# Experts with few rows: float32 weights used as loaded, two 64-column products side by side

## The chip, the cores and the metric

The kernel runs on one core of a Trainium2 chip. The metric is the device time of one execution in microseconds: the median of three runs is 1269.22 us (1267.71 to 1270.82).

## What is computed

One decoder layer on 1024 tokens of width 1024. The part that matters here is the last one, a mixture of 32 experts. Each token is sent to two experts; the kernel computes only those rows. All arithmetic is to float32 accuracy.

```python
def hier_moe(h, rg_w, rg_b, re_w, re_b, w_gate, w_up, w_down):
    ...                                   # group top-1, then expert top-2 inside it
    y = jnp.zeros_like(h)
    for e in range(N_EXPERTS):            # 32 experts
        he = jax.nn.silu(h @ w_gate[e]) * (h @ w_up[e])   # (1024 x 256) each
        y = y + comb[:, e:e + 1] * (he @ w_down[e])       # (256 x 1024)
    return y
```

One expert's weights are 1024x256 (gate), 1024x256 (up) and 256x1024 (down), 3 MB in float32.

## The kernel before

Attention, gating and the output product come first (lines 155 to 1090). The expert part, `moe` (line 1574), works through 35 units: the 32 experts, those after the sixth sorted by how many tokens they have, and a second half unit for the three experts in `PAIRS`. A unit has 128 slots for tokens, or 64 if it is a second half or its expert is one of the 13 in `SMALLS` (9, 11, 13, ... 29, 30, 31). Units 0 to 8 all have 128 slots; from expert 9 on, large and small ones alternate.

A unit goes like this. GpSimd gathers the token rows by an indirect DMA (`gather`). TensorE transposes them and `tokens` splits them into a high and a low part: ScalarE writes `xh` as float32r (a shortened float32), VectorE the rest `xl`. `gate_up` multiplies by gate and up weights, `down` by the down weights, ScalarE scales the result into `y`, and GpSimd adds it to the rows of `acc` in memory by an accumulating indirect DMA (`scatter`).

Weights come in pieces of 128x1024 values, 0.5 MB: four for gate and up together, two for down, so 192 for the experts. `plan` (line 155) lists them with the engines of their split, `fetch` loads a piece on the SP queue into a page `wr`, `presplit` splits it into two pages, `wh` and `wl` (`split`, line 138: line 132 or 136 writes the high part on ScalarE or GpSimd, line 140 the low part on VectorE or GpSimd). With a piece given as "a", ScalarE writes `wh` and VectorE `wl`. Down pieces of experts 0 to 27 go by `DOWN = "gp"`: for the first GpSimd writes `wh` and VectorE `wl`, for the second ScalarE writes `wh` and GpSimd `wl`. The pages come from one pool of 41; a load waits on the SP queue until a page is free.

A product of two split numbers takes three float32r matmuls (`mm3`, line 143). In a unit of 64 slots `xh` and `xl` stand beside each other as 128 columns, so two matmuls do for `gate_up`: all 128 columns by `wh` (line 1495) and the 64 of `xh` by `wl` (line 1494), 16 for the eight blocks of 128; the two halves are added while they are turned (line 1506). `down` takes 12 in either kind of unit.

The last two experts (30, 31) don't scatter: their results stay in SBUF and are added by matmuls in `finish` (line 1699). The order on each engine is set by the framework's scheduler, from the order of the code and its own costs; pools and semaphores decide the rest.

Of the kernel before, what the change touches and what calls it, by code (L numbers as in the profile page):

```python
# [10 lines left out]
F32 = mybir.dt.float32  # L11
F32R = mybir.dt.float32r
BF16 = mybir.dt.bfloat16
I32 = mybir.dt.int32
U32 = mybir.dt.uint32
AF = mybir.ActivationFunctionType
ALU = mybir.AluOpType
# [72 lines left out]
class Kern:  # L90
# [25 lines left out]

    def era(self):

        return self.const.tile([P, 448], F32, name=self.name("era"), tag="era")

    def temp(self, shape, dt):

# [32 lines left out]
    def plan(self):  # L155
        I = self.I
        win = I["w_in"][0]
        W = []

        def cols(src, kt, c0, w, eng="a", k0=0):  # L160
            ap = src[k0 * P : (k0 + kt) * P, c0 : c0 + w].rearrange("(k p) c -> p k c", p=P)
            W.append(([P, kt, w], lambda t: [self.nc.sync.dma_start(t, ap)], eng))

        cols(win, KT, C_KI, 72, "q")
        for j in range(4):
            cols(win, KT, C_QI + j * P, P, self.QI[j])
# [12 lines left out]
        for j in range(4):
            cols(win, KT, C_Q + j * P, P)  # L180
        for d in range(4):
            cols(I["w_proj_a"][0], 4, d * 256, 256)
        kw = D // self.OW
        for c in range(D // self.OW):
            for j in range(KT // kw):
                cols(I["w_out"][0], kw, c * self.OW, self.OW, "a", j * kw)

        def gu(get):
            for j in range(4):

                def ld(t, j=j):
                    wg, wu, _ = get()
                    for z, w in enumerate((wg, wu)):
                        self.nc.sync.dma_start(t[:, :, z * 256 : (z + 1) * 256], w[j * 256 : (j + 1) * 256, :].rearrange("(k p) f -> p k f", p=P))

                W.append(([P, 2, 512], ld, "a"))

        def dn(get, eng):
            for f in range(2):
                W.append(([P, D], lambda t, f=f: self.nc.sync.dma_start(t, get()[2][f * P : (f + 1) * P, :]), eng[f]))  # L200

        gets = [self.expert(e) if e < FIXED else self.ordered(e) for e in range(NE)]
        self.units = [(e, z) for e in range(NE) for z in range(1 + (e in PAIRS))]
        for what, u in self.sequence():
            e, z = self.units[u]
            if z == 0 and what == "gu":
                gu(gets[e])
            elif z == 0:
                dn(gets[e], self.DOWN if e < NE - self.LAST else "aa")
        self.W = W  # L210
        self.raws, self.hls = [], []
        self.pos = 0
        self.urgent = {}
        self.LD, self.LS = self.EARLY_LD, 1
# [43 lines left out]
    def presplit(self, n):  # L258
        n = min(n, len(self.W))
        self.fetch(n)  # L260
        while len(self.hls) < n:
            i = len(self.hls)
            shape, _, eng = self.W[i]
            h = self.page(shape, F32R, "wh")
            l = self.page(shape, F32R, "wl")
            with ExitStack() as es:
                for ins in self.urgent.values():
                    es.enter_context(self.tc.issue_after(ins))
                self.split(eng, h, l, self.raws[i])
            self.raws[i] = None  # L270
            self.hls.append((h, l))
# [658 lines left out]
    def merge(self):  # L930
# [38 lines left out]
        self.acc = self.dram.tile([T, D], F32, name="acc")  # L969
        late = self.era()  # L970
        self.lg = late[:, : 8 * 40].rearrange("p (t c) -> p t c", t=8)
        self.olists = late[:, 8 * 40 :].rearrange("p (z e) -> p z e", z=4)
        self.r2 = self.cst([P, 8], F32, "r2")
        ss = self.small([P, 8, NC], F32, "ss2", bufs=1)
        xs = []
# [112 lines left out]
    ROUTE_PAGES = (1, 0)  # L1088
    RINGS = (3, 1, 2)
    WRITES = ["scalar"] * 13 + ["sync"] * 3  # L1090
    DOWN, LAST = "gp", 4
    XAHEAD = 4
    EARLYFETCH = {(1, 0): 12, (1, 2): 16, (1, 4): 22, (1, 6): 28}
    EARLYSPLIT = {(1, 2): 4}
# [4 lines left out]
    def router_consts(self):  # L1099
# [26 lines left out]
        self.islot, _ = iota("islot", [P, P], [[1, P]])  # L1126
        self.itile, _ = iota("itile", [P, 8], [[128, 8]])
        self.icol, _ = iota("icol", [P, 1], [[0, 1]], cm=1)

        self.places = self.cst([NE, 2, NE], F32, "places")  # L1130
        for z in range(2):
# [183 lines left out]
    def order(self):  # L1315

        nc, bc = self.nc, self.bc
        V = nc.vector
        t = self.arena()
        nt = self.ps1([P, NE + 1], "nt", tag="a")  # L1320
        nc.tensor.matmul(nt[:, :NE], lhsT=self.oneb, rhs=self.Mc[:, 8, :], start=True, stop=True)
        nc.tensor.matmul(nt[:NE, NE:], lhsT=self.Mc[:, 8, :], rhs=self.oneb[:, 0:1], start=True, stop=True)
        key, more, PO = t([P, NE]), t([P, NE]), t([P, NE])
        own, rank, rows = t([P, 1]), t([P, 1]), t([P, 1])
        e = slice(0, NE)
        dyn, tie, fixed = (self.cols[:, z : z + 1] for z in range(3))

        V.scalar_tensor_tensor(key, nt[:, :NE], float(NE), self.ties, op0=ALU.mult, op1=ALU.add)
        V.tensor_tensor(key, key, self.dyn, ALU.mult)
        V.scalar_tensor_tensor(own[e], nt[e, NE:], float(NE), tie, op0=ALU.mult, op1=ALU.add)  # L1330
        V.tensor_scalar(more[e], key[e], own[e], None, op0=ALU.is_gt, op1=ALU.add, accum_out=rank[e])
        V.tensor_scalar(rank[e], rank[e], dyn, fixed, op0=ALU.mult, op1=ALU.add)
        V.tensor_scalar(PO[e], self.places[:, 0, :], rank[e], None, op0=ALU.is_equal)

        ep = self.ps1([1, NE], "eid", tag="a")
        nc.tensor.matmul(ep, lhsT=self.icol[e], rhs=PO[e], start=True, stop=True)
        self.eid = self.cst([1, NE], I32, "eid")
        V.tensor_copy(self.eid, ep)
        V.tensor_copy(rows[e], nt[e, NE:])
        self.ordered_state = rows[e], rank[e], PO[e]  # L1340
        yield

        tp = self.ps1([NE, 3, P], "lt", tag="a")
        for z in range(3):
            nc.tensor.transpose(tp[:, z, :], self.lists[:, z, :], self.ident)
        lt = self.page([NE, 5, P], F32, "lt")
        nc.scalar.activation(lt[:, :3], tp, AF.Copy)

        for z in range(2):
            nc.scalar.activation(lt[:, 3 + z].rearrange("e (r s) -> e r s", r=2), tp[:, 1 - z, :HALF].unsqueeze(1).to_broadcast([NE, 2, HALF]), AF.Copy)  # L1350
        op = self.ps1([P, 5, NE], "ol", tag="a")
        for z in range(5):
            nc.tensor.matmul(op[:, z, :], lhsT=lt[:, z, :], rhs=PO[:NE], start=True, stop=True)
        o = self.olists
        self.tokp = self.cst([P, NE], I32, "tokp")
        V.tensor_copy(self.tokp, op[:, 0, :])
        V.tensor_copy(o, op[:, 1:5])
        self.rsp, self.wsp, self.rsd, self.tokd = (o[:, z, :] for z in range(4))
        yield

    def route_overflow(self):
# [103 lines left out]
    def tokens(self, xg):  # L1465
# [14 lines left out]
        self.hurry("x", *self.lastsplit)  # L1480
        return (x2.rearrange("p k r s -> p k (r s)"),) if m == HALF else (xh, xl)

    def gate_up(self, x, r, piece):

        nc = self.nc
        pp = self.ps1([P, 512], "gu", tag="b")
        half = len(x) == 1
        for j in range(4):
            h, l = piece()
            for k in (2 * j, 2 * j + 1):  # L1490
                if half:
# [66 lines left out]

    def scatter(self, tok, y):

        self.nc.gpsimd.indirect_dma_start(out=self.acc, out_offset=bass.IndirectOffsetOnAxis(ap=tok, axis=0), in_=y[: tok.shape[0]], in_offset=None, bounds_check=T - 1, oob_is_err=False, compute_op=ALU.add)  # L1561

    def spread(self, places):

# [9 lines left out]
    def moe(self):  # L1574
# [5 lines left out]
        def lists(u):  # L1580
            e, z = units[u]
            if z:
                c = slice(PAIRS.index(e), PAIRS.index(e) + 1)
                return self.tok2[:HALF, c], self.rs2d[:, c], self.ws2[:HALF, c]
            if e in SMALLS:
                return self.tokp[: LIMITS[e], e : e + 1], self.rsd[:, e : e + 1], self.wsp[:HALF, e : e + 1]
            if e < FIXED:
                return tuple(v[:, e : e + 1] for v in (self.tok, self.rs, self.ws))
# [19 lines left out]

        self.xring = [[self.page([P, KT, P], F32R, n) for n in ("xh", "xl")] for _ in range(2)]
        self.yring = []  # L1610
        X, G = {}, {}
        seq = self.sequence()
        rows, ys = [], []
        ovf = self.route_overflow()
        for step in range(n + 2):
# [9 lines left out]
                u = len(rows)  # L1625
                rows.append(self.gather(self.tok[:, u : u + 1] if u < FIXED else lists(u)[0], self.xg[u % self.NXG][: halves(u) * HALF]))
            if step < n:
                X[step] = self.tokens(rows[step])
            if step == 0:
                self.route_factors()  # L1630
                order = self.order()
# [3 lines left out]
            while seq and seq[0][1] < step - (seq[0][0] == "dn") and seq[0][1] in (X if seq[0][0] == "gu" else G):  # L1635
                what, u = seq.pop(0)
                tok, r, ws = lists(u)
                if what == "gu":
                    G[u] = self.gate_up(X.pop(u), r, pieces(u, what))
                    continue  # L1640
                if u == n - self.SPREAD:
                    self.kept = self.spread((NE - 2, NE - 1))
# [134 lines left out]
```

## Time and profile before

| what | value |
|---|---|
| median of 3 runs | 1269.22 us |
| profiled execution | 1266.41 us, its span 1264.6 us |
| TensorE busy in the span | 1141.6 us (90%) |
| VectorE busy | 985.7 us (78%) |
| ScalarE busy | 608.9 us (48%) |
| GpSimd busy | 443.2 us (35%) |
| memory traffic | 190.69 MB in packets, 151 GB/s on average |
| mean granted TensorE clock | 0.962 of full speed |

Busy times count compute instructions only. Matmul ends are modelled and overlap the next start, so what one matmul costs is read from the distance of two starts. In the names, the tile before the arrow is written by those behind it; `wr`, `wh`, `wl` are pages of weights, `xt`, `xh`, `xl` the tokens of a unit, `gu` and `y` its two products in PSUM, `kb` small tiles between the two, `gut` and `ht` the turned gate and up values. A waiting engine is shown with what released it last.

### The profile page before, as it was taken

The page shows a single profiled execution, that of the slowest core. Times are in us where ns is not written, and L with a number is a line of the kernel's source. Part 1 is how long each engine was busy: PE and PEld are TensorE (multiplying, and loading weights), DVE is VectorE, ACT ScalarE, POOL GpSimd, SP SyncE. Part 2 cuts the span into 40 slices and gives each one's busy share as a digit, 9 for nine tenths or more (in the row PEclk, how much of TensorE's full clock was granted, in tenths as well). Part 3 has the DMA queues.
Part 4 walks back from the last instruction along what each step waited for, and adds up shares of the span by engine and source line. Part 5 has one row for each costly group of instructions (what it writes and reads, how often), then busy time and mean ns, then how long its engine had stood idle before and what let it go on. Part 6 is the DMA issues. An engine that isn't in the chain of part 4 may idle for free.

```text
span 1264.6 us, 17817 instructions
## 1 busy us (share of the span) xinstructions
PE 1141.6 (90%) x5892; PEld 922.0 (73%) x5892; DVE 985.7 (78%) x1724; ACT 608.9 (48%) x1048; POOL 443.2 (35%) x406
## 2 busy tenths in 40 slices
PE   4999999989999989899999899877988788999993
PEld 3789888878888867799888788755765555666662
DVE  7444988999999994798888713768999879777875
ACT  6324642222222214687773413236657465666773
POOL 5100141510111110344425412235675784675511
PEclk7999999999999999999999999979899899999997
DMA  7301031312322220000047647868799788998936
GB/s 216 84 17 51 1 84 34 100 51 86 107 74 84 80 70 18 1 2 1 1 143 232 237 139 282 270 222 258 242 282 268 242 254 264 290 326 250 313 113 241
DMA packets 148144, 190.69 MB, mean 151 GB/s; under 512 B 16514, under 2 KB 119466, under 8 KB 148051
## 3 DMA queue, kind: packets, MB, share of 16 engines
q1 hardware_dynamic: 134226, 156.85, 38.5%
q0 software_dynamic: 8784, 21.16, 7.0%
q10 hardware_dynamic: 5040, 11.54, 2.4%
q8 instruction: 47, 0.77, 0.3%
q14 instruction: 47, 0.38, 0.1%
HBM read 164.61 MB, written 33.07 MB: 156 GB/s over the span
## 4 chain that ended last, share of the span: by engine, by line
PE 53%; DVE 24%; issue 7%; DMA 6%; ACT 5%; POOL 3%; SPq 1%; DVEq 0%; POOLq 0%; ACTq 0%
DVE wl L140 6%; PE pj L145 6%; PE pj L147 6%; PE pj L146 6%; DVE junk L546 5%; DMA wr<-w_up 4%; PE xo L146 2%; PE xo L147 2%; PE xo L145 2%; DVE S L878 2%; PE y L147 2%; PE y L145 2%; PE gu L146 2%; PE y L146 2%; PE gu L1495 1%
## 5 line engine op out<-in xcount | busy, mean ns | idle before, releaser
L140 DVE TENSOR_TENSOR wl<-wr,wh 128x1024 fp32r<-128x1024 f32 x212 | 327.2, 1561 | 46.3 <-ACT wh L132 25.8
L132 ACT ACTIVATE wh<-wr 128x1024 fp32r<-128x1024 f32 x206 | 212.1, 1054 | 60.4 <-PE pj L146 28.5
L546 DVE TENSOR_SCALAR_CACHE_REDUCE junk<-idx,cand 128x384 bf16<-128x384 f32 (+2 forms) x198 | 187.0, 944 | 6.8 <-POOL idx L509 1.0
L145 PE MATMUL pj<-hT,wh 128*128 128x512 f32 (+1 forms) x464 | 179.8, 387 | 2.5 <-ACT wh L132 2.5
L147 PE MATMUL pj<-hT,wl 128*128 128x512 f32 (+1 forms) x464 | 178.6, 385 | 0.0
L146 PE MATMUL pj<-hT,wh 128*128 128x512 f32 (+1 forms) x464 | 178.3, 384 | 0.0
L145 PEld LDWEIGHTS pj<-hT,wh 128*128 128x128 f32 x464 | 88.0, 190 | 20.1 <-ACT wh L132 2.7
L147 PEld LDWEIGHTS pj<-hT,wl 128*128 128x128 f32 x464 | 87.9, 190 | 16.8
L146 PEld LDWEIGHTS pj<-hT,wh 128*128 128x128 f32 x464 | 87.8, 189 | 16.7
L140 POOL TENSOR_TENSOR wl<-wr,wh 128x1024 fp32r<-128x1024 f32 (+1 forms) x30 | 85.7, 2856 | 13.8 <-ACT wh L132 12.8
L146 PE MATMUL gu<-wl,xh 128*128 128x512 f32 x152 | 65.5, 431 | 21.4 <-DVE wl L140 21.3
L711 POOL TENSOR_TENSOR yt<-yt,sb 128x1024 f32<-128x1024 f32 x8 | 20.1, 2512 | 169.7 <-ACT sb L719 169.7
L886 POOL TENSOR_SCALAR P<-P,pair 128x128 f32<-128x128 f32 (+3 forms) x64 | 48.1, 752 | 88.1 <-DVE pair L885 77.9
L136 POOL TENSOR_SCALAR wh<-wr 128x1024 fp32r<-128x1024 f32 (+1 forms) x36 | 48.4, 1346 | 54.8 <-ACT kih L457 17.4
L719 ACT ACTIVATE sb<-pj 128x512 f32<-128x512 f32 x32 | 19.0, 594 | 100.5 <-PE pj L147 100.5
L1561 POOL DMA_INDIRECT acc<-y,tokp x24 | 47.2, 1966 | 52.3 <-ACT y L1551 23.5
L145 PE MATMUL gu<-wh,xh 128*128 128x512 f32 x152 | 63.6, 418 | 1.0 <-ACT wh L132 0.7
L147 PE MATMUL y<-wh,kb 128*128 128x512 f32 (+1 forms) x140 | 58.7, 420 | 4.1 <-DVE kb L140 4.1
L147 PE MATMUL gu<-wh,xl 128*128 128x512 f32 x152 | 62.2, 409 | 0.0
L145 PE MATMUL y<-wh,kb 128*128 128x512 f32 (+1 forms) x140 | 59.1, 422 | 3.4 <-ACT kb L132 2.1
L146 PE MATMUL y<-wl,kb 128*128 128x512 f32 (+1 forms) x140 | 58.2, 416 | 0.0
L506 DVE SCALAR_TENSOR_TENSOR idx<-rl,era,idx 128x384 f32<-128x384 f32 (+5 forms) x42 | 39.8, 947 | 20.1 <-ACT rl L502 18.9
(434 smaller groups left out, 2904.2 us busy)
## 6 DMA issues: line engine op xcount, KB each, us to landing
wr<-w_gate SPq DMA_DIRECT2D x128, 256.0 KB, 5.3
wr<-w_up SPq DMA_DIRECT2D x128, 256.0 KB, 5.7
wr<-w_down SPq DMA_DIRECT2D x64, 512.0 KB, 5.7
wr<-w_in SPq DMA_DIRECT2D x33, 512.0 KB, 4.3
x<-x SPq DMA_DIRECT2D x8, 512.0 KB, 7.2
sga<-sb ACTq DMA_DIRECT2D x8, 512.0 KB, 4.5
ybg<-yt POOLq DMA_DIRECT2D x8, 512.0 KB, 3.3
ybr<-ybg SPq DMA_DIRECT2D x8, 512.0 KB, 4.2
```

What stands on the lines that cost most here:

```text
L132: return nc.scalar.activation(out, src, AF.Copy)
L136: return nc.gpsimd.tensor_scalar(out, src, 1.0, 0.0, op0=ALU.mult, op1=ALU.add)
L140: b = (self.nc.gpsimd if eng in "pq" else self.nc.vector).tensor_tensor(l, src, h.bitcast(F32), ALU.subtract)
L145: nc.tensor.matmul(out, lhsT=sh, rhs=mh, start=start, stop=False)
L146: nc.tensor.matmul(out, lhsT=sh, rhs=ml, start=False, stop=False)
L147: self.lastmm = nc.tensor.matmul(out, lhsT=sl, rhs=mh, start=False, stop=stop)
L506: nc.vector.scalar_tensor_tensor(acc, rl, wv, acc, op0=ALU.mult, op1=ALU.add)
L546: nc.vector.tensor_scalar(junk[:, : (j + 3) * P], self.idx[j + 2][:, : (j + 3) * P], cf[:, j : j + 1], None, op0=op, op1=ALU.add, accum_ou ...
L711: nc.gpsimd.tensor_tensor(yt, yt, sb, ALU.mult)
L878: nc.vector.tensor_tensor_reduce(out=s3, in0=s3, in1=m.rearrange("p (c w) -> p c w", c=nch), scale=-0.125, scalar=-NEG, op0=ALU.add, op1=A ...
L886: nc.gpsimd.tensor_scalar(p, p, sm[:, 1:2], 0.0, op0=ALU.mult, op1=ALU.add)
L1561: self.nc.gpsimd.indirect_dma_start(out=self.acc, out_offset=bass.IndirectOffsetOnAxis(ap=tok, axis=0), in_=y[: tok.shape[0]], in_offset=N ...
```

## The change

Small units no longer split their weights. `plan` gives their pieces the engine None, and `presplit` then hands out the loaded page itself. `tokens_small` writes the tokens once, in float32. `gate_up` has a new branch: for each of the eight blocks one float32 matmul of 64 columns, the even blocks into partitions 0 to 63 of the result, the odd ones into 64 to 127, in the left and the right half of the array; the halves are added as before. `down_small` does the same for the down weights, the two halves being the two halves of the 1024 result columns. So `y` of such a unit is 128 partitions of 512 values, and `scatter` adds it to half rows of `acc`, with a list of half rows `tokh`. This holds for gate and up of all 13 experts in `SMALLS`; for down of 11, without experts 30 and 31, whose down pieces stay split.

The down pieces of all other experts are now split by ScalarE and VectorE ("aa"); GpSimd splits no weights of experts.

```diff
@@ plan
-                W.append(([P, 2, 512], ld, "a"))
+                W.append(([P, 2, 512], ld, eng))
...
-                gu(gets[e])
+                gu(gets[e], None if e in SMALLS else "a")
             elif z == 0:
-                dn(gets[e], self.DOWN if e < NE - self.LAST else "aa")
+                dn(gets[e], (None, None) if e in SMALLS and e < NE - 2 else "aa")
@@ presplit
             shape, _, eng = self.W[i]
+            if eng is None:
+                self.hls.append(self.raws[i])
+                self.raws[i] = None
+                continue
@@ order (lists of tokens per unit)
+        self.tokh = self.cst([P, NE], I32, "tokh")
+        V.tensor_scalar(self.tokh, self.tokd, 2.0, self.below, op0=ALU.mult, op1=ALU.add)
@@ new
+    def tokens_small(self, xg):
...
+        for k in range(KT):
+            self.lastpe = nc.tensor.transpose(tp[:, k, :], xg[:, k * P : (k + 1) * P], self.ident[:HALF, :HALF])
+        a = nc.scalar.activation(x, tp, AF.Copy)
...
+    def down_small(self, wslot, sg, piece):
...
+        for f in range(2):
+            w = piece()
+            for c in range(2):
+                nc.tensor.matmul(yp[c * HALF : (c + 1) * HALF], lhsT=sg[:, f, :], rhs=w[:, c * 512 : (c + 1) * 512], start=(f == 0), stop=(f == 1))
...
+        y = self.rot("y", self.yring)[:, :512]
+        self.hurry("y", nc.scalar.activation(y, yp, AF.Copy, scale=wslot).ins)
@@ gate_up
+            if whole:
+
+                w = piece()
+                for k in range(2):
+                    nc.tensor.matmul(pp[k * HALF : (k + 1) * HALF], lhsT=x[0][:, 2 * j + k, :], rhs=w[:, k, :], start=(j == 0), stop=(j == 3))
+                continue
@@ scatter
-        self.nc.gpsimd.indirect_dma_start(out=self.acc, ...
+        parts = D // y.shape[1]
+        acc = self.acc.rearrange("t (z c) -> (t z) c", z=parts)
+        self.nc.gpsimd.indirect_dma_start(out=acc, ..., bounds_check=T * parts - 1, ..., compute_op=ALU.add)
@@ moe
+        xs = self.page([P, 2, KT, HALF], F32, "xs")
+        self.xsmall = [xs[:, z] for z in range(2)]
...
+                if units[u][0] in SMALLS and u < n - 2:
+                    e = units[u][0]
+                    ys.append((self.tokh[:, e : e + 1], self.down_small(ws, G.pop(u), pieces(u, what))))
```

TensorE's queue between the first two small units, before: the `y` products of the first (expert 9; rows with 64x512), then the `gu` of the second. Numbers behind names tell tiles apart.

```order
L145 MATMUL y_8793<-wh_8738,kb_8789 64x512
L146 MATMUL y_8793<-wl_8739,kb_8789 64x512
L147 MATMUL y_8793<-wh_8738,kb_8790 64x512
...
L1478 MATMUL xt_8848<-identr,h_1126_6546 128x128 x4
L1495 MATMUL gu_8855<-wh_8764,xh_7520 128x512
L1497 MATMUL gu_8855<-wl_8765,xh_7520 64x512
L1494 MATMUL gu_8855<-wl_8765,xh_7520 64x512
L1495 MATMUL gu_8855<-wh_8764,xh_7520 128x512
L1494 MATMUL gu_8855<-wl_8777,xh_7520 64x512
L1495 MATMUL gu_8855<-wh_8776,xh_7520 128x512
```

The same place after the change (L1509 is the small `y`, L1527 the small `gu`, and x2 stands for the left and the right half of the array):

```order
L146 MATMUL y_8663<-wl_8620,kb_8656 128x512
L1509 MATMUL y_8754<-wr_8329,kb_8647 64x512 x2
L1509 MATMUL y_8754<-wr_8352,kb_8647 64x512 x2
L147 MATMUL y_8663<-wh_8619,kb_8657 128x512
...
L1486 MATMUL xt_8793<-identr,h_1126_6548 128x128 x4
L1527 MATMUL gu_8800<-wr_8364,xs_7524 64x512 x2
L1527 MATMUL gu_8800<-wr_8422,xs_7524 64x512 x2
L1527 MATMUL gu_8800<-wr_8435,xs_7524 64x512 x2
L1527 MATMUL gu_8800<-wr_8459,xs_7524 64x512 x2
L145 MATMUL gu_8892<-wh_8816,xh_7520 128x512
```

Sixteen rows of `gu` have become eight, twelve of `y` four, and they read `wr`; the left product always stands directly ahead of the right one of its pair, and the small `y` has moved into the middle of the preceding large one.

GpSimd's queue in the first units, before: splits (`wh`, `wl`), gathers (from `h2d`) and scatters (into `acc`) take turns.

```order
L136 TENSOR_SCALAR wh_7857<-wr_7120 128x1024
L1462 DMA h_1126_6546<-h2d,tokp 128x1024
L1561 DMA acc<-y_7832,tok 1024x1024
L140 TENSOR_TENSOR wl_7871<-wr_7122,wh_7870 128x1024
L136 TENSOR_SCALAR wh_7966<-wr_7299 128x1024
L1462 DMA h_1127_6547<-h2d,tokp 128x1024
L1561 DMA acc<-y_7833,tok 1024x1024
```

GpSimd's queue there after the change:

```order
L1470 DMA h_1126_6548<-h2d,tokp 128x1024
L1603 DMA acc<-y_7839,tok 1024x1024
L1470 DMA h_1127_6549<-h2d,tokp 128x1024
L1603 DMA acc<-y_7840,tok 1024x1024
L1470 DMA g_1119_6537<-h2d,tokp 128x1024
L1603 DMA acc<-y_7841,tok 1024x1024
```

Only gathers and scatters are left; the splits stand on ScalarE's and VectorE's queues.

## Rows read from the trace of the kernel before

**Rows 1.** Stretches of the expert part: length, busy us (instructions), clock, DMA share, GB/s.
```profile
862.00:966.00 104.00, 87.19 (x394) 66.48 (x392) 97.71 (x96) 67.37 (x87) 65.29 (x36) 0.95 0.86 259
966.00:1080.00 114.00, 92.92 (x428) 65.01 (x425) 96.19 (x104) 68.41 (x92) 79.35 (x53) 0.93 0.87 256
1080.00:1200.00 120.00, 112.21 (x546) 78.87 (x547) 91.64 (x91) 79.50 (x110) 74.32 (x42) 0.99 0.95 295
1200.00:1232.00 32.00, 29.14 (x145) 19.49 (x144) 23.85 (x29) 24.92 (x33) 5.50 (x5) 1.00 0.40 114
```
**Rows 2.** ScalarE's timeline: `y` of units 0, 8 and 34 (start, us).
```profile
862.00 1.12 ACT L1551 ACTIVATE y<-y,lists 128x1024 f32<-128x1024 f32 x1 [1.19 <-PE y L147]
965.65 1.12 ACT L1551 ACTIVATE y<-y,era 128x1024 f32<-128x1024 f32 x1 [0.23 <-PE y L147]
1229.89 1.11 ACT L1545 ACTIVATE yh<-y,era 64x1024 fp32r<-64x1024 f32 x1 [1.65 <-PE y L147]
```
**Rows 3.** Waits of TensorE, 862 to 966: us in total, times, longest.
```profile
PE gu L146 <- DVE wl L140: 12.5, 7, 3.1
PE gu L1497 <- DVE wl L140: 3.7, 1, 3.7
```
**Rows 4.** Waits of the SP queue, which issues the weight loads, 862 to 966.
```profile
SPq L194 <- DVE wl L140: 17.2, 7, 6.7
SPq L200 <- DVE wl L140: 13.5, 5, 3.9
```
**Rows 5.** VectorE's timeline in that stretch: two splits of one form.
```profile
863.53 1.23 DVE L140 TENSOR_TENSOR wl<-wr,wh 128x1024 fp32r<-128x1024 f32 x1 [0.95 <-POOL wh L136]
...
867.38 4.74 DVE L140 TENSOR_TENSOR wl<-wr,wh 128x1024 fp32r<-128x1024 f32 x1 [0.26 <-ACT wh L132]
```
**Rows 6.** GpSimd's timeline at the same place.
```profile
868.09 2.94 POOL L140 TENSOR_TENSOR wl<-wr,wh 128x1024 fp32r<-128x1024 f32 x1
```
**Rows 7.** Groups by form, 800 to 1265: count, busy us, mean ns, idle before.
```profile
L140 DVE TENSOR_TENSOR wl<-wr,wh 128x1024 fp32r<-128x1024 f32 x160 | 254.6, 1613 | 38.0 <-ACT wh L132 19.7 <-POOL wh L136 15.6 <-DMA wr<-w_up 1.9
L132 ACT ACTIVATE wh<-wr 128x1024 fp32r<-128x1024 f32 x160 | 164.1, 1053 | 16.3 <-DVE wl L140 9.7 <-POOL wl L140 2.6 <-PE gu L1494 2.2
L140 POOL TENSOR_TENSOR wl<-wr,wh 128x1024 fp32r<-128x1024 f32 x28 | 81.9, 2925 | 13.7 <-ACT wh L132 12.8 <-PE y L147 0.4 <-POOL wh L136 0.2
...
L136 POOL TENSOR_SCALAR wh<-wr 128x1024 fp32r<-128x1024 f32 x28 | 37.6, 1344 | 22.5 <-PE gu L146 10.2 <-PE y L146 8.4 <-DVE wl L140 3.6
```
**Rows 8.** DMA queues, 780 to 1265: packets, MB, share of 16 engines.
```profile
q1 hardware_dynamic: 75652, 102.85, 63.9%
q0 software_dynamic: 7632, 16.96, 15.8%
```
**Rows 9.** TensorE's timeline in a small unit's `gu` (start, us).
```profile
1139.74 0.39 PE L1495 MATMUL gu<-wh,xh 128*128 128x512 f32 x1
1139.96 0.40 PE L1494 MATMUL gu<-wl,xh 128*64 128x512 f32 x1
1140.20 0.39 PE L1495 MATMUL gu<-wh,xh 128*128 128x512 f32 x1
```
**Rows 10.** TensorE's timeline in `finish`: float32 (L1739, two records each) between float32r.
```profile
1243.36 1.02 PE L1739 MATMUL fin<-xf,identr 128*128 128x512 f32 x2
1243.82 0.79 PE L1741 MATMUL fin<-yh,S 128*128 128x512 f32 x1
1244.45 0.39 PE L1741 MATMUL fin<-yl,S 128*128 128x512 f32 x1
1244.67 1.02 PE L1739 MATMUL fin<-xf,identr 128*128 128x512 f32 x2
```
**Rows 11.** The SP queue's timeline: the last weight loads.
```profile
1192.84 9.73 SPq L200 DMA_DIRECT2D wr<-w_down  x6
```
**Rows 12.** Waits of the SP queue, 1080 to 1200.
```profile
SPq L200 <- PE gu L147: 6.4, 5, 2.3
SPq L200 <- PE y L147: 6.0, 4, 2.7
```

More of the change, by code (lines that the diff above doesn't have):

```diff
@@ L117, in era @@
     def era(self):
-        return self.const.tile([P, 448], F32, name=self.name("era"), tag="era")
+        return self.const.tile([P, 480], F32, name=self.name("era"), tag="era")
     def temp(self, shape, dt):
@@ L186, in plan, with gu @@
                 cols(I["w_out"][0], kw, c * self.OW, self.OW, "a", j * kw)
-        def gu(get):
+        def gu(get, eng):
             for j in range(4):
@@ L971, in merge @@
         self.lg = late[:, : 8 * 40].rearrange("p (t c) -> p t c", t=8)
-        self.olists = late[:, 8 * 40 :].rearrange("p (z e) -> p z e", z=4)
+        self.olists = late[:, 8 * 40 :].rearrange("p (z e) -> p z e", z=5)
         self.r2 = self.cst([P, 8], F32, "r2")
@@ L1090 @@
     WRITES = ["scalar"] * 13 + ["sync"] * 3
-    DOWN, LAST = "gp", 4
     XAHEAD = 4
@@ L1128, in router_consts @@
         self.icol, _ = iota("icol", [P, 1], [[0, 1]], cm=1)
+        self.below = self.cst([P, 1], F32, "below")
+        nc.vector.tensor_scalar(self.below, self.icol, float(HALF), None, op0=ALU.is_ge)
         self.places = self.cst([NE, 2, NE], F32, "places")
@@ L1345, in order @@
             nc.tensor.transpose(tp[:, z, :], self.lists[:, z, :], self.ident)
-        lt = self.page([NE, 5, P], F32, "lt")
+        lt = self.page([NE, 6, P], F32, "lt")
         nc.scalar.activation(lt[:, :3], tp, AF.Copy)
[L1349 to L1352, printed above, removed]
+        for z in range(3):
+            nc.scalar.activation(lt[:, 3 + z].rearrange("e (r s) -> e r s", r=2), tp[:, (1, 0, 2)[z], :HALF].unsqueeze(1).to_broadcast([NE, 2, HALF]), AF.Copy)
+        op = self.ps1([P, 6, NE], "ol", tag="a")
+        for z in range(6):
             nc.tensor.matmul(op[:, z, :], lhsT=lt[:, z, :], rhs=PO[:NE], start=True, stop=True)
@@ L1356, in order @@
         V.tensor_copy(self.tokp, op[:, 0, :])
-        V.tensor_copy(o, op[:, 1:5])
-        self.rsp, self.wsp, self.rsd, self.tokd = (o[:, z, :] for z in range(4))
+        V.tensor_copy(o, op[:, 1:6])
+        self.rsp, self.wsp, self.rsd, self.tokd, self.wsd = (o[:, z, :] for z in range(5))
+        self.tokh = self.cst([P, NE], I32, "tokh")
+        V.tensor_scalar(self.tokh, self.tokd, 2.0, self.below, op0=ALU.mult, op1=ALU.add)
         yield
@@ L1481, in tokens @@
         return (x2.rearrange("p k r s -> p k (r s)"),) if m == HALF else (xh, xl)
+    def tokens_small(self, xg):
+        nc = self.nc
+        x = self.rot("xs", self.xsmall)
+        tp = self.ps1([P, KT, HALF], "xt", tag="a")
+        for k in range(KT):
+            self.lastpe = nc.tensor.transpose(tp[:, k, :], xg[:, k * P : (k + 1) * P], self.ident[:HALF, :HALF])
+        a = nc.scalar.activation(x, tp, AF.Copy)
+        self.hurry("x", a.ins)
+        return (x,)
+    def down_small(self, wslot, sg, piece):
+        nc = self.nc
+        yp = self.ps2("y")[:, 0, :]
+        for f in range(2):
+            w = piece()
+            for c in range(2):
+                nc.tensor.matmul(yp[c * HALF : (c + 1) * HALF], lhsT=sg[:, f, :], rhs=w[:, c * 512 : (c + 1) * 512], start=(f == 0), stop=(f == 1))
+        while len(self.yring) < self.NY:
+            self.yring.append(self.page([P, D], F32, "y"))
+        y = self.rot("y", self.yring)[:, :512]
+        self.hurry("y", nc.scalar.activation(y, yp, AF.Copy, scale=wslot).ins)
+        return y
     def gate_up(self, x, r, piece):
@@ L1487, in gate_up @@
         half = len(x) == 1
+        whole = half and x[0].shape[2] == HALF
         for j in range(4):
+            if whole:
[3 more added lines that the diff above has]
+                continue
             h, l = piece()
@@ L1559, in scatter @@
     def scatter(self, tok, y):
-        self.nc.gpsimd.indirect_dma_start(out=self.acc, out_offset=bass.IndirectOffsetOnAxis(ap=tok, axis=0), in_=y[: tok.shape[0]], in_offset=None, bounds_check=T - 1, oob_is_err=False, compute_op=ALU.add)
+        parts = D // y.shape[1]
+        acc = self.acc.rearrange("t (z c) -> (t z) c", z=parts)
+        self.nc.gpsimd.indirect_dma_start(out=acc, out_offset=bass.IndirectOffsetOnAxis(ap=tok, axis=0), in_=y[: tok.shape[0]], in_offset=None, bounds_check=T * parts - 1, oob_is_err=False, compute_op=ALU.add)
     def spread(self, places):
@@ L1585, in lists @@
             if e in SMALLS:
+                if e < NE - 2:
+                    return self.tokp[: LIMITS[e], e : e + 1], self.rsd[:, e : e + 1], self.wsd[:, e : e + 1]
                 return self.tokp[: LIMITS[e], e : e + 1], self.rsd[:, e : e + 1], self.wsp[:HALF, e : e + 1]
@@ L1627, in moe @@
             if step < n:
-                X[step] = self.tokens(rows[step])
+                X[step] = (self.tokens_small if units[step][0] in SMALLS else self.tokens)(rows[step])
             if step == 0:
@@ L1639, in moe @@
                     G[u] = self.gate_up(X.pop(u), r, pieces(u, what))
+                    continue
+                if units[u][0] in SMALLS and u < n - 2:
+                    e = units[u][0]
+                    ys.append((self.tokh[:, e : e + 1], self.down_small(ws, G.pop(u), pieces(u, what))))
+                    while len(ys) > (self.LATE if u < n - 3 else 0):
+                        self.scatter(*ys.pop(0))
                     continue
```

## Prediction

> **What bounds the kernel now.** I read the span by stages first. The change touches only the expert part, from the first `y` at 862 us to the last at about 1230 [rows 2], with loads running ahead of it and 35 us of `finish` behind. Units 0 to 8, all large, need 965.65 − 862.00 = 103.7 us, 13.0 us each; the other 26 need 264.2 us, 10.2 us each. In the first stretch VectorE is busy 97.7 of 104 us, TensorE 87, and the DMA engines have a share of 0.86. In the last long stretch, 1080 to 1200, VectorE is down to 91.6 of 120, TensorE at 112.2, the DMA share at 0.95 [rows 1]. So early units wait for VectorE, late ones for TensorE and for memory together.
>
> Next, who waits for whom. In the first stretch TensorE waits 12.5 + 3.7 us for low parts of weights (line 140 on VectorE) [rows 3], and the SP queue waits 17.2 + 13.5 us for the same line, because a page is free for the next load only when it has been split [rows 4]. VectorE is slow for a reason that the timeline shows: the same subtraction takes 1.23 us alone and 4.74 us where GpSimd's own low-part split (2.94 us) runs beside it [rows 5, 6]. Over all 160 splits the mean is 1.61 us [rows 7].
>
> Last, what memory would allow. Between 780 and 1265 the load queue moved 102.85 MB in 63.9% of 485 us, 332 GB/s while at work; gathers and scatters 16.96 MB in 15.8%, 221 GB/s [rows 8]. The bytes stay the same, so the engines' busy time does too: 0.86·104 + 0.87·114 + 0.95·120 = 303 us in the 338 us from 862 to 1200 [rows 1]. The weights can't arrive sooner than their share lets them. The last load instructions leave the SP queue at 1192.8 to 1202.6 [rows 11].
>
> **The change part by part.**
>
> *Splits.* Unsplit are 13·4 gate and up pieces and 11·2 down pieces, 74. VectorE takes 46 low parts fewer: it had 64 of these 74 (10 were GpSimd's), and gets 18 second down pieces of large experts, the rest of GpSimd's 28 [rows 7]. ScalarE takes 46 high parts fewer by the same count. GpSimd drops 28 + 28 splits, 81.9 + 37.6 us [rows 7]. VectorE's 114 splits that are left cost 1.23 us each if nobody runs beside them: 140 us in place of 254.6. The early large units get one split more on each of ScalarE and VectorE: VectorE pays 6·1.23 = 7.4 us per unit in place of 5·1.61 = 8.1; ScalarE 1.05 us per unit more [rows 7], on 67 busy of 104 us [rows 1]. Both are below the 13 us of a unit. TensorE's 16 us of waits and SP's 31 us should mostly go. Late next is memory, since TensorE's work in a large unit is 36 matmuls at 0.23 us (the distance of two starts [rows 9]), 8.3 us, plus turns.
>
> *Products of a small unit.* Before: 16 in `gu` and 12 in `y`, 28·0.23 = 6.4 us. After: 8 and 4 float32 ones. One float32 product of 512 columns costs 0.85 us: from 1243.36 to 1244.67 there are 1.31 us for it and two float32r ones of 0.23 [rows 10]; its weight loads are in that price, so none is added. Side by side, a pair of two 64-column products costs 0.85, so six pairs 5.1 us, 1.3 us less than before; one behind the other 1.7, so 10.2 us, 3.8 more. For 11 units with both products and two with `gu` alone (3.4 or 6.8 us against 3.7) that is −15 us or +48 us of TensorE's time. No row of before shows two 64-column products in the two halves of the array. I take 0.85, since the nearest rows show products in the array together: each has a record of 0.39 us and the next starts after 0.23 [rows 9]; and I keep both ends.
>
> The Trainium skill's TensorEngine Tiling (Array Packing), under Key Properties, says that tiles of the array work independently and run matmuls in parallel; by that the pair costs 0.85 us and the saving stands; no row here shows it. The same list says that a change of tiling mode drains the engine. Against that rule the rows show 128-column and 64-column products taking turns 0.22 to 0.24 us apart, with no drain between [rows 9]. If the rule held, and a switch cost the 0.16 us by which a record exceeds the distance of starts, some four switches in each of 13 units would add 8 us to TensorE; by the rows, nothing.
>
> *Smaller edits.* One ScalarE copy in place of a copy and a subtraction for the tokens, a `y` of 128x512 in place of 64x1024, no split between the two products: all shorten a small unit's chain, on engines with room. The scatter of 11 units goes by rows of 2 KB in place of 4 KB. Their slots are at most 540 rows, 2.2 MB, 10 us at 221 GB/s; if half rows moved at half the pace this adds 10 us of DMA time, if only bytes count nothing. I take nothing, since the load queue moves its packets, mean 1.4 KB, at 332 GB/s [rows 8]. One more page is held for good out of 41, but a small piece takes one page where it took three. The list `tokh` costs one matmul, one copy and two short VectorE instructions, once.
>
> **The sum**, against the profiled execution of 1266.4 us. What the kernel has shown it can hold for 120 us is a DMA share of 0.95. If the two earlier stretches come to that, they shrink to 104·0.86/0.95 = 94.1 and 114·0.87/0.95 = 104.4 us: −9.9 and −9.6. The stretch at 0.95 gains nothing, though TensorE does less there. Behind the stream, the `y` of expert 29 is 1 us shorter. Together −20.5, 1245.9 us. The median of the runs shown is 2.8 us above the profiled execution, so I forecast 1249; its own range is 1238 to 1260.
>
> **Rivals.**
> *One behind the other (slower).* The two halves don't run at once: the change then doesn't do what its words say. TensorE gets 48 us more between 966 and 1232, where it is busy 234 of 266 us. If all 32 idle us took it up, the end comes 16 us later; if it keeps the 6.5% idle of its best stretch [rows 1], 282/0.935 = 302 us, 36 later. Less the 9.9 us of the first stretch: +6 to +26, 1275 to 1295 as a median, most likely 1287. It decides from a pair of about 1.3 us on: there the 74 pairs cost 96 us in place of 78, and the 18 us added eat the gain. For it: each of the pair streams 512 columns of its own, and nothing in this trace shows two such products at once. Against it: nothing in the program puts a wait between them.
> *Memory full.* The share goes to 1.00 in all three stretches: 303 us in place of 338, −35, and 2 us off the backlog behind: about 1232. For it: VectorE and GpSimd no longer hold pages back. Against: even from 1080 to 1200 the SP queue waited for pages that TensorE had not released [rows 12].
> *Hidden.* The first stretch gets faster by using up pages loaded ahead, and later units wait for memory instead; the end moves by 0 to 5 us: 1264 to 1269. For it: the late stretch is already at 0.95. Against: SP's 31 us of waits for splits are time in which loads could have been sent.
>
> **How the numbers follow.** Forecast 0.45, memory full 0.17, hidden 0.12, one behind the other 0.24, other ways to be slower 0.02. What a measurement of this kernel can tell from no change is about 0.3%, 3.8 us. Faster is the first two and half of hidden: 0.67; same 0.07; slower 0.26. The range must reach into the case of serial products: 1222 to 1290, from memory full with a shorter tail to the middle of that rival.
>
> **What would show it.** Right: VectorE's splits at 1.2 us everywhere, none above 2; pairs of line 1527 starting 0.85 us after one another; the DMA share in the first units at 0.95; no wait for line 140 in the SP queue's first places. Wrong: starts of pairs 1.7 us apart, TensorE busy to the brim after 966 and the DMA share below 0.85 there; or units 0 to 8 still taking 13 us each, which would say that VectorE was not what held the loads.

## The result, and the profile after

The changed kernel takes 1222.91 us (median of 4 runs, 1222.13 to 1224.43) against 1268.47 us for the kernel before on the same chip: the ratio is 0.9641, with a 95% interval of 0.9622 to 0.9659. The direction was the forecast one and the time lies inside the range, but the gain is 45.6 us where 20.5 were worked out, more than twice as much.

The stages of the profiled execution after (1223.43 us, span 1221.5), with the columns of [rows 1]: length, busy us and instructions of TensorE, its weight loads, VectorE, ScalarE and GpSimd, then clock, DMA share (the mean busy share of the 16 DMA engines, as the profile counts it) and GB/s. In the rows below PE is TensorE, DVE VectorE, ACT ScalarE, POOL GpSimd, and SPq the SP queue.

```profile
862.00:943.00 81.00, 79.57 (x376) 59.29 (x376) 70.61 (x97) 67.94 (x88) 30.12 (x17) 1.00 1.00 305
943.00:1000.00 57.00, 48.54 (x228) 28.97 (x223) 28.80 (x45) 28.09 (x40) 23.12 (x27) 0.88 1.06 319
1000.00:1060.00 60.00, 58.58 (x307) 37.16 (x306) 31.22 (x46) 32.48 (x47) 16.19 (x12) 1.00 1.03 333
1060.00:1140.00 80.00, 78.60 (x399) 49.47 (x397) 35.64 (x44) 39.92 (x59) 21.69 (x17) 1.00 1.04 336
1140.00:1180.00 40.00, 34.07 (x163) 18.89 (x162) 9.55 (x14) 17.60 (x27) 11.11 (x8) 0.91 0.43 112
```

From 862 to 1140 the DMA share stands at 1.00 or above in every stretch. Length by rate, the four stretches moved 24.7 + 18.2 + 20.0 + 26.9 = 89.8 MB in 278 us, 323 GB/s; before, [rows 1] gives 26.9 + 29.2 + 35.4 = 91.5 MB in the 338 us up to 1200, 271 GB/s. Nearly the same bytes came in 60 us less. The clock granted over the whole run is no part of the gain: 0.962 before, 0.966 after.

ScalarE's `y` of units 0, 8 and 34, which answer to [rows 2]:

```profile
860.83 1.12 ACT L1591 ACTIVATE y<-y,lists 128x1024 f32<-128x1024 f32 x1 [1.18 <-PE y L147]
...
946.44 1.12 ACT L1591 ACTIVATE y<-y,era 128x1024 f32<-128x1024 f32 x1 [0.88 <-PE y L147]
...
1176.20 1.11 ACT L1585 ACTIVATE yh<-y,era 64x1024 fp32r<-64x1024 f32 x1 [1.67 <-PE y L147]
```

The 43.1 us between the two spans split like this: 1.2 before the first `y`; units 0 to 8 in 85.6 us in place of 103.7, −18.0; the other 26 in 229.8 in place of 264.2, −34.5; and behind the last `y` 45.3 us in place of 34.7, +10.6. (The small `y` of unit 9 now stands ahead of that of unit 8, so the 85.6 us hold it too.) The loads of `acc` for `finish` show the longer tail: before, they begin 0.6 us ahead of the last `y`, now 9.8 us behind it.

```profile
1229.30 5.24 SPq L1707 DMA_DIRECT2D xf<-acc  x8
...
1186.03 3.70 SPq L1759 DMA_DIRECT2D xf<-acc  x8
```

The waits of the SP queue from 862 to 1140 (us in total, times, longest) answer to [rows 4] and [rows 12]:

```profile
SPq L194 <- DMA wr<-w_down: 16.5, 18, 1.8
SPq L194 <- PE gu L147: 13.1, 12, 2.9
SPq L194 <- DMA wr<-w_gate: 12.1, 22, 2.1
SPq L200 <- DMA wr<-w_gate: 9.8, 18, 1.8
```

Before, that queue waited for pages that VectorE or TensorE still held: of 183 us of waits from 862 to 1200 only 6.7 ended with a load that landed. Now 55.4 of 102.5 us do, these lines and others together: for a good half of the waiting, loads stand ready and memory is late.

VectorE's splits from 800 on, by form (answers to [rows 7]), all at the time of one alone in [rows 5]:

```profile
L140 DVE TENSOR_TENSOR wl<-wr,wh 128x1024 fp32r<-128x1024 f32 x114 | 136.2, 1220 | 71.2 <-ACT wh L132 50.9 <-DMA wr<-w_down 5.7 <-DMA wr<-w_gate 4.5
```

TensorE at two small units: first the eight float32 products of a `gu` (16 records), then the four of a `y` (8 records), each with the next start.

```profile
1031.37 3.65 PE L1527 MATMUL gu<-wr,xs 128*64 128x512 f32 x16
1034.95 0.50 PE L145 MATMUL gu<-wh,xh 128*128 128x512 f32 x1
1035.29 0.40 PE L146 MATMUL gu<-wl,xh 128*128 128x512 f32 x1
...
1043.07 1.94 PE L1509 MATMUL y<-wr,kb 128*64 128x512 f32 x8
1044.93 0.50 PE L147 MATMUL y<-wh,kb 128*128 128x512 f32 x1
```

Four pairs in 3.58 us and two in 1.86: 0.90 to 0.93 us a pair, against 0.85 worked out for one product of this size. So the pairs do run side by side. The Trainium skill (TensorEngine Tiling (Array Packing), Key Properties) says that tiles execute in parallel; this trace agrees. Its rule that a mode switch drains the array shows in no more than a few hundredths of a microsecond: the first wide product behind the pairs is followed after 0.34 us in place of 0.23, but the same distance is 0.31 behind turns of `ht`, which use the whole array as the wide products do:

```profile
872.73 0.38 PE L1567 MATMUL ht<-identr,kb 128*128 128x128 f32 x2
872.87 0.47 PE L146 MATMUL gu<-wl,xh 128*128 128x512 f32 x1
873.18 0.39 PE L147 MATMUL gu<-wh,xl 128*128 128x512 f32 x1
```

### The profile page after: what moved, and what is told of

Its sections match the earlier page's. It is cut to its first block, busy times and chain, and to the rows that moved or that the text cites. A ratio compares the mean times of both kernels' runs of the same rounds, so it can differ in the third digit from the quotient of the medians.

```text
span 1221.5 us, 17405 instructions
## 1 busy us (share of the span) xinstructions
PE 1119.8 (92%) x5850; PEld 886.8 (73%) x5850; DVE 850.3 (70%) x1656; ACT 557.0 (46%) x992; POOL 318.4 (26%) x350
## 5 line engine op out<-in xcount | busy, mean ns | idle before, releaser
L140 DVE TENSOR_TENSOR wl<-wr,wh 128x1024 fp32r<-128x1024 f32 x166 | 208.5, 1275 | 79.8 <-ACT wh L132 57.2
L132 ACT ACTIVATE wh<-wr 128x1024 fp32r<-128x1024 f32 x160 | 164.5, 1055 | 60.7 <-PE pj L146 28.5
L146 PE MATMUL gu<-wl,xh 128*128 128x512 f32 x152 | 63.0, 415 | 0.4
L888 ACT ACTIVATE P<-S,pair 128x128 f32<-128x128 f32 (+3 forms) x64 | 47.4, 741 | 15.4 <-DVE pair L889 6.8
L506 ACT ACTIVATE rl<-ix 128x384 f32<-128x384 f32 (+5 forms) x48 | 35.7, 760 | 38.9 <-PE ix L501 34.9
L145 PE MATMUL xo<-wh,m 128*128 128x512 f32 x128 | 51.4, 401 | 2.1 <-ACT m L132 1.7
L140 DVE TENSOR_TENSOR pt<-pt,pt 128x128 fp32r<-128x128 f32 (+2 forms) x96 | 50.6, 548 | 2.5 <-ACT pt L132 1.8
L147 PE MATMUL xo<-wh,m 128*128 128x512 f32 x128 | 50.2, 392 | 1.0 <-DVE m L140 1.0
L146 PE MATMUL xo<-wl,m 128*128 128x512 f32 x128 | 50.7, 396 | 0.0
```

The source lines that it names most:

```text
L132: return nc.scalar.activation(out, src, AF.Copy)
L140: b = (self.nc.gpsimd if eng in "pq" else self.nc.vector).tensor_tensor(l, src, h.bitcast(F32), ALU.subtract)
L145: nc.tensor.matmul(out, lhsT=sh, rhs=mh, start=start, stop=False)
L146: nc.tensor.matmul(out, lhsT=sh, rhs=ml, start=False, stop=False)
L147: self.lastmm = nc.tensor.matmul(out, lhsT=sl, rhs=mh, start=False, stop=stop)
L506: nc.scalar.activation(r3, ps[:, :nch, :w], AF.Relu)
```

## Experiments

Each run is compared with the kernel before on its own chip. Four questions: which part of the change gave the gain, what bounds the kernel now, what GpSimd's splits cost, and what holds the end.

| run | median us | ratio to before, 95% interval |
|---|---|---|
| the change | 1222.91 | 0.9641 [0.9622, 0.9659] |
| e1_no_gp | 1220.78 | 0.9628 [0.9598, 0.9659] |
| e2_gp_kept | 1241.74 | 0.9797 [0.9763, 0.983] |
| e3_one_half | 1260.66 | 0.9956 [0.9934, 0.9979] |
| e6_less_pe | 1218.26 | 0.9618 [0.9586, 0.965] |
| e7_low_only | 1238.85 | 0.9744 [0.9708, 0.978] |
| e7_high_only | 1234.29 | 0.9728 [0.9702, 0.9754] |
| e5_bytes | 1206.03 | 0.9504 [0.948, 0.9529] |
| e8_earlier0 | 1223.88 | 0.964 [0.9614, 0.9667] |
| e9_pairs_after | 1223.0 | 0.9634 [0.96, 0.9668] |
| e9_pairs_e1 | 1216.24 | 0.9581 [0.9543, 0.962] |
| e10_two_fewer | 1215.92 | 0.9582 [0.9548, 0.9617] |

**Which part.** The first run takes from the change only that GpSimd leaves the splits.

```diff
-    DOWN, LAST = "gp", 4
+    DOWN, LAST = "aa", 4
```

> The kernel before, with one edit: GpSimd splits no expert weights (all down pieces go to ScalarE and VectorE); small experts stay split. Theory A (GpSimd's splits blocked VectorE's, which held back pages and loads; the rest of the change matters little): VectorE's splits at 1.2 us, DMA share near 1.0 from 862 on, at least 30 of the 45 us, 1223 to 1238 us. Theory B (the unsplit small weights did it: one page in place of three and 46 splits fewer): at most 15 us, 1253 to 1268, with the DMA share after 966 still about 0.9.

1220.78 us: all of the gain, 2 us more than theory A allowed, with the small weights still split and no float32 product. In the time of the whole kernel theory A holds. Its stretches, same columns as above:

```profile
862.00:943.00 81.00, 75.08 (x348) 58.34 (x347) 75.02 (x101) 71.03 (x91) 31.38 (x17) 0.96 0.99 303
943.00:1000.00 57.00, 50.94 (x239) 37.91 (x238) 51.40 (x65) 43.87 (x58) 31.02 (x28) 0.92 0.96 290
1000.00:1060.00 60.00, 60.00 (x311) 44.76 (x310) 51.90 (x69) 50.70 (x67) 21.98 (x13) 0.99 1.02 324
1060.00:1140.00 80.00, 78.48 (x411) 58.45 (x411) 61.64 (x73) 63.72 (x87) 26.16 (x18) 1.00 1.05 339
```

VectorE works 240 us here where the changed kernel needs 166, and the DMA share is near 1.0 all the same. The waits of the load queue don't tell the two kernels' bounds apart: here 37 of 124 us end with a load that landed, and most of the others with a page that TensorE held.

The course is not the same up to the end, though. The last weight loads of this run and its last `y`, with the last loads of the changed kernel between them:

```profile
1150.34 3.49 SPq L200 DMA_DIRECT2D wr<-w_down  x3
...
1136.38 4.39 SPq L200 DMA_DIRECT2D wr<-w_down  x6
...
1184.84 1.11 ACT L1545 ACTIVATE yh<-y,era 64x1024 fp32r<-64x1024 f32 x1 [2.08 <-PE y L147]
```

With unsplit weights the loads are through 13 us sooner, and the last `y` comes 8.6 us sooner (1176.20). Behind it the changed kernel needs 45.3 us, this run 36.4, and so both spans are 1221 us. So the rest of the change, unsplit weights and their products, does speed the units up, and the tail takes it back; what holds that tail comes below.

The second run is the opposite: small weights unsplit, GpSimd kept.

```diff
-                dn(..., (None, None) if e in SMALLS and e < NE - 2 else "aa")
+                dn(..., (None, None) if e in SMALLS and e < NE - 2 else "gp" if e < NE - 4 else "aa")
```

> The changed kernel, with one edit: the down pieces of the 18 large experts below 28 are again split half by GpSimd, as before. Theory A: most of the gain is lost, 1250 us or more, units 0 to 8 again at 13 us each. Theory B: the first nine units fall back to 13 us (about 20 us lost there), but the DMA share after them is 1.0 and part of that is won back: 1225 to 1240 us.

1241.74 us, between the two theories' numbers and nearest to B's upper end; the course is B's: units 0 to 8 take 105.7 us, the other 26 take 227.8. Up to 943 the DMA share is 0.87 as before, and behind it above 1.0:

```profile
862.00:943.00 81.00, 70.20 (x314) 52.62 (x312) 75.17 (x61) 51.45 (x66) 56.77 (x32) 0.96 0.87 258
943.00:1000.00 57.00, 50.58 (x224) 32.29 (x224) 37.36 (x64) 29.81 (x39) 31.73 (x32) 0.91 1.04 319
```

So this kernel is 26 us ahead of the one before, all from unit 9 on; GpSimd's leaving alone is worth 47; both together 45. The 26 us are not shown to be the unsplit weights' alone: from unit 9 on GpSimd makes 18 splits here where it made 38 before, and no run parts the two. What is shown is that the gains don't add up in the time of the whole kernel.

**What bounds the changed kernel.** Two runs add or take TensorE's work and leave the weight loads as they are. In the first, both products of a pair go to the same half of the array, and `y` is scattered in whole rows.

```diff
-  nc.tensor.matmul(pp[k * HALF : (k + 1) * HALF], lhsT=x[0][:, 2 * j + k, :], rhs=w[:, k, :], start=(j == 0), stop=(j == 3))
+  nc.tensor.matmul(pp[:HALF], lhsT=x[0][:, 2 * j + k, :], rhs=w[:, k, :], start=(j + k == 0), stop=(j + k == 4))
...
-  nc.tensor.matmul(yp[c * HALF : (c + 1) * HALF], lhsT=sg[:, f, :], rhs=w[:, c * 512 : (c + 1) * 512], ...)
+  nc.tensor.matmul(yp[:, c, :], lhsT=sg[:, f, :], rhs=w[:, c * 512 : (c + 1) * 512], ...)
```

> The changed kernel, with the two products of a pair in the same half of the array, one behind the other (same weights, same loads, y of 64x1024 as before). By the starts in the changed kernel a pair costs 0.85 us side by side; here it should cost 1.7, 48 us more of TensorE's time over 74 pairs. If TensorE bounds the changed kernel (it is busy 299 of the 318 us from 862 to 1180), 30 to 48 us slower than it, 1253 to 1271. If memory bounds it (DMA share 1.0 or more from 862 to 1060), the added work sits partly beside the loads: 5 to 25 us slower, 1228 to 1248.

1260.66 us, 38 slower than the change, with the same work in its `gu` and `y`:

```profile
1024.63 7.08 PE L1527 MATMUL gu<-wr,xs 128*64 128x512 f32 x16
1040.32 3.65 PE L1509 MATMUL y<-wr,kb 128*64 128x512 f32 x8
```

7.08 us in place of 3.65, 3.65 in place of 1.94. Run singly, float32 products would lose nearly all of the gain. The 48 us in the expectation are too few: they are what serial products cost over the kernel before; over the change, 74 pairs at 0.86 us more (a pair takes 1.75 from start to start, 7.01 us for four) are 64. So 38 of 64 us reach the end, less than a kernel bound by TensorE throughout would show. The next run removes work from it.

```diff
-  self.mm3(pp, x[0][:, k, :], x[1][:, k, :], h[:, k % 2, :], l[:, k % 2, :], k == 0, k == KT - 1)
+  self.mm2(pp, x[0][:, k, :], h[:, k % 2, :], l[:, k % 2, :], k == 0, k == KT - 1)   # without xl by wh
...
-  self.mm3(yp[:, c, :], hh[:, f, :], hl[:, f, :], h[:, cs], l[:, cs], f == 0, f == 1)
+  self.mm2(yp[:, c, :], hh[:, f, :], h[:, cs], l[:, cs], f == 0, f == 1)
```

> The changed kernel without the third product (low part of the tokens or of the gated values by the high part of the weights) in the 128-slot units and in the split down products: 228 products of 0.23 us fewer in the 19 large units, 52 us off TensorE, all loads as they are. If memory bounds the changed kernel: 0 to 12 us faster, 1211 to 1223, the last weight load leaving at about 1140 as in it. If TensorE does: 30 to 50 us faster, 1173 to 1193.

1218.26 us: some 52 us of products less are worth 4.7, and by the two ratios' intervals even that is not clear of noise. In the profile the granted clock is lower (0.945 for 0.966), and TensorE is busy only 35 us less from 862 to 1180 (263.9 for 299.4). The first nine units gain by it, 78.2 us for 85.6. The weight stream doesn't: its last loads leave the SP queue 279 us after the first `y` (858.39), where the change needs 280.

```profile
1133.35 4.12 SPq L205 DMA_DIRECT2D wr<-w_down  x6
```

The third run takes bytes and no products.

```diff
-  self.nc.sync.dma_start(t, get()[2][f * P : (f + 1) * P, :])
+  self.nc.sync.dma_start(t[:, :512], get()[2][f * P : (f + 1) * P, :512])   # where eng[f] is None
...
-  nc.tensor.matmul(yp[c * HALF : (c + 1) * HALF], lhsT=sg[:, f, :], rhs=w[:, c * 512 : (c + 1) * 512], ...)
+  nc.tensor.matmul(yp[c * HALF : (c + 1) * HALF], lhsT=sg[:, f, :], rhs=w[:, :512], ...)
```

> The changed kernel, with half of each of the 22 unsplit down pieces left unloaded (the first 512 columns are loaded and used for both halves of the result): 5.8 MB fewer at the same number of matmuls, 17 us of DMA time at 332 GB/s. If memory bounds the changed kernel: 8 to 17 us faster, 1206 to 1215 us. If TensorE does, as its busy share of 0.94 would have it: 0 to 4 us, 1219 to 1223, since no product goes. If the end is held by the chain of scatters (the last five wait one for another from 1161 to 1186): also under 4 us, with the last y earlier than 1176.

1206.03 us, 17 faster: nearly every microsecond of DMA time removed comes off the end. Memory bounds the changed kernel's stream of units. TensorE is close behind (busy 79.6 of 81 us in the first stretch), so added work shows and removed work hardly does.

**What GpSimd's splits cost.** The kernel before, with only the low or only the high parts left to GpSimd (`DOWN` "ap" and "ga").

> The kernel before, where GpSimd keeps only its low parts (the subtraction of the second down piece, 28 times 2.9 us) and ScalarE takes the high part of the first. Theory A1 (the subtraction on GpSimd and the subtraction on VectorE shut each other out): nearly all of the loss stays, 1250 to 1268 us, VectorE's mean split at 1.5 us or more. Theory A2 (what costs is time on GpSimd's queue, in which gathers and scatters stand behind splits): the loss goes with GpSimd's time, 82 of 120 us, so about 1253; here both agree, and the next run parts them.

> The kernel before, where GpSimd keeps only its high parts (the copy of the first down piece, 28 times 1.3 us) and VectorE takes the low part of the second. A1: a copy reads one operand and hardly blocks VectorE; 1221 to 1228 us, VectorE's mean split at 1.25. A2: GpSimd is still busy 38 us more than without splits, in front of gathers and scatters: 1230 to 1240.

1238.85 and 1234.29 us: the first is faster than either theory allowed, the second fits A2. Without the low parts or without the high ones, most of the gain is there. The groups by form, low only ahead of high only:

```profile
L140 DVE TENSOR_TENSOR wl<-wr,wh 128x1024 fp32r<-128x1024 f32 x160 | 234.1, 1486 | 34.9 <-ACT wh L132 28.9 <-ACT junk L1503 2.5 <-ACT y L1551 1.8
L140 POOL TENSOR_TENSOR wl<-wr,wh 128x1024 fp32r<-128x1024 f32 x28 | 75.9, 2731 | 13.7 <-ACT wh L132 13.5
```

```profile
L140 DVE TENSOR_TENSOR wl<-wr,wh 128x1024 fp32r<-128x1024 f32 x188 | 244.1, 1329 | 30.3 <-ACT wh L132 15.6 <-POOL wh L136 11.0 <-ACT junk L1503 1.8
L136 POOL TENSOR_SCALAR wh<-wr 128x1024 fp32r<-128x1024 f32 x28 | 47.7, 1703 | 28.2 <-PE y L146 6.3 <-PE gu L146 6.2 <-DVE wl L140 5.5
```

The first experiment's, without either:

```profile
L140 DVE TENSOR_TENSOR wl<-wr,wh 128x1024 fp32r<-128x1024 f32 x188 | 228.7, 1244 | 39.6 <-ACT wh L132 36.4 <-DMA wr<-w_up 2.0 <-DMA wr<-w_gate 0.5
```

VectorE's mean split is 1.49 us beside GpSimd's subtractions and 1.33 beside its copies, against 1.24 there, so it is slower beside either. The Trainium skill (SBUF — State Buffer, Who interferes with whom) says that GpSimd and VectorE share a pair of ports, that a VectorE instruction with two SBUF inputs contends with a GpSimd one that reads SBUF, and that the loser is blocked; the means agree. In [rows 5, 6] VectorE's split is the longer one although it is recorded 0.7 us ahead of GpSimd's, so which of the two waits for the other can't be read from those rows. Against the kernel without GpSimd's splits the low parts alone cost 18 us, the high ones alone 13.5, both 47: more than the sum. Why, no run settles; that a kernel at the edge of its memory hides the first microseconds of a delay is argued, not shown. Nor is the path of the loss settled. Slower splits are one. Against A2's gathers speaks that in the kernel before TensorE has no wait for a gathered row from 862 to 1232. But GpSimd's queue delays VectorE in a second way: VectorE sits idle for high parts that GpSimd has yet to write, 15.6 us before [rows 7] and 11.0 in the second of these runs.

**What holds the end.** GpSimd's timeline shows the last scatters of the changed kernel (experts 26, 27, 28, the second half of 28, and 29):

```profile
1161.06 1.86 POOL L1603 DMA_INDIRECT acc<-y,tokp  x1 [4.93 <-ACT y L1591]
1167.07 1.55 POOL L1603 DMA_INDIRECT acc<-y,tokh  x1 [4.16 <-ACT y L1591]
1171.52 1.55 POOL L1603 DMA_INDIRECT acc<-y,tokp  x1 [2.89 <-ACT warm L1573]
1178.39 1.43 POOL L1603 DMA_INDIRECT acc<-y,tok  x1 [5.32 <-issue]
1182.31 1.60 POOL L1603 DMA_INDIRECT acc<-y,tokh  x1 [1.83 <-DMA acc<-y,tok]
```

Only in the last row is the scatter before named as what released it. ScalarE's timeline tells for the others; it has the `y` of experts 27, 28, the second half of 28, and 29:

```profile
1160.68 0.68 ACT L1513 ACTIVATE y<-y,era 128x512 f32<-128x512 f32 x1
...
1165.83 1.12 ACT L1591 ACTIVATE y<-y,era 128x1024 f32<-128x1024 f32 x1 [4.46 <-PE y L147]
...
1168.68 1.11 ACT L1591 ACTIVATE y<-y,ws 64x1024 f32<-64x1024 f32 x1
...
1171.40 0.67 ACT L1513 ACTIVATE y<-y,era 128x512 f32<-128x512 f32 x1
```

These four `y` were done 4.6 to 10.2 us before their scatters began, so it was the scatter before that each waited for. The loads of `acc` for `finish` follow at 1186.03, 10 us after the last `y` has begun. One run leaves out the last two scatters:

> The changed kernel without the scatters of its last two scattering units (the second half of expert 28, and expert 29; their results are left out of the sum). Theory T: the loads of acc begin some 7.5 us earlier, when the scatter of expert 28 has landed (1178.4), and the end comes 6 to 8 us earlier, 1215 to 1217. Theory S, or an end held by the last product at 1177 and what follows it: 0 to 3 us.

The loads began at 1179.04 and the kernel took 1215.92 us, 7.0 less, as the chain would have it. Two attempts to shorten it with the whole result computed failed. With `EARLIER = 0`:

> The changed kernel, with the gate and up products of the last unit (expert 31) one place later in the order, behind the down products of expert 29, the last that scatters. If the chain of scatters holds the end: the y of expert 29 comes 3 us earlier, but its scatter waits for the three before it, so 0 to 3 us faster, 1220 to 1223. If TensorE's last product does: 0 to 4 us slower, as the last unit's chain has less beside it.

1223.88 us, no difference; the `y` of expert 29 stayed where it was (1171.21 against 1171.40), so the run tells nothing of the chain. With `PAIRS = (18, 22, 26)` in place of `(20, 24, 28)`, in the changed kernel and in the first experiment's:

> The changed kernel, with the three experts that have a second half unit at places 18, 22 and 26 in place of 20, 24 and 28, so that the last large unit is smaller and no half unit stands in the last four. Theory T (in the changed kernel the end is held by the chain of its last five scatters, 1161 to 1186, while its last y is done at 1177): the chain is one shorter, 3 to 8 us faster, 1215 to 1220. Theory S (the end follows the weight stream, wherever the units stand): within 2 us of the changed kernel.

> The same move of the pairs on the first experiment's kernel (split small weights, no split on GpSimd). There the last y ended at 1186 and the loads of acc began at 1185.5, so its end is held by products, not by scatters. Theory T: within 2 us of 1221, so the changed kernel with the move is 3 to 8 us ahead of it, which is what the unsplit products are worth once the scatters let it through. Theory S: the two stay equal.

Theory T failed in both, and S in the second. The changed kernel stayed at 1223.0, as S has it: its last five scatters ran from 1162.8 to 1187.8, as late as without the move. The kernel with split weights came to 1216.24, 4.5 less than without the move, though the intervals of the two overlap. This is the fastest version that computes the whole result, 0.9581 of before; it has two edits, and no unsplit weight. It was not run beside the change itself on one chip, and their intervals end within 0.0002 of each other. Beside the changed kernel with the same move, on the same chip, it is 6.8 us faster, and the times of the two don't overlap (1213.02 to 1218.80, 1221.76 to 1224.85).

## Why the prediction was wrong

**The step that failed** is the sum's ceiling for memory: "What the kernel has shown it can hold for 120 us is a DMA share of 0.95 ... The stretch at 0.95 gains nothing". That stretch was itself held back, by the page waits of [rows 12], which I had read and used only against the rival. A share seen while the queue waits for pages is no ceiling. Once pages came in time the share was 1.00 to 1.06 for 278 us, and the late units gained as the early ones did: 34.5 us from unit 9 on, where 9.6 were forecast. Even the rival "memory full" was too small, at −35 for the loads: it took 1.00 as the most that a share can be, and 302 GB/s per full share ([rows 1]: 91.5 MB in 303 us) where 313 came (89.8 MB in 286, the 278 us weighted by their shares). The pace of the load queue itself was right: 75.93 MB at a share of 81.9% of 278 us, 333 GB/s, beside the 332 of [rows 8]. That the time still lies inside the range is luck: its lower end was set for a full memory with a shorter tail, and the tail got longer.

**Right**, by the runs: that GpSimd's splits, which slow VectorE's, held the loads back, and that their end would let the first nine units go (−18.0 us, forecast −9.9); VectorE's split without GpSimd, 1.22 us; the price of a pair and that it runs side by side, 0.90 us for 0.85; that memory is late next.

**Wrong beside that**: the slower rival was priced at 1275 to 1295; the third experiment, whose products run one behind the other, took 1260.66, below the kernel before, since the loads gained there too. The tail was taken as 1 us shorter; it is 10.6 us longer, because the last `y` come 54 us sooner and bunched (those of the last five scatters within 11.7 us), and their scatters wait one for another. And the sum took both parts of the change together; the first experiment gets the whole gain from one.

## What to carry to other kernels

A busy share read while the engine's own queue waits for something else is a floor of what the resource can do; price its ceiling by the bytes over the pace at work, and check what the queue waited for. When a change has two parts that feed the same wait, undo each alone: here one line gave all of the gain that the whole rewrite had. And compare the two kernels' courses, not only their ends: what the rewrite won over that line by its last `y` it lost in the tail. Work on GpSimd that reads SBUF had a price on VectorE's timeline here, so a split that GpSimd "helps" with can cost more than VectorE doing it all.

## What was not expected of the hardware

Accumulating scatters into one tensor ran one behind the other at the end, and how long each took went with what it carried, read from the next start in the chain: up to 128 rows of 4 KB in 6.9 us (1171.52 to 1178.4), up to 64 rows of 4 KB in 3.9 (1178.39 to 1182.31). By `LIMITS` experts 27 and 29 have at most 36 and 32 tokens; their half rows of 2 KB, two for a token, took about 4.4 us (1167.07 to 1171.5) and 3.6 (1182.31 to the loads of `acc` at 1185.9). The scatter of expert 29 by whole rows, in the kernel before, took as long: 3.6 us from 1225.73 to the loads of `acc` at 1229.30. So half rows as such were neither quicker nor slower. The DMA share of a stretch can exceed 1.00 in the profile: it was 1.06 over 57 us.
